# A neighbour sum on one core: the first sort's masks, casts and counts in another order

## The chip, the cores and the metric

The kernel runs on one core of one Trainium2 chip. The metric is the device time of one execution in microseconds (us). The engines are PE (matrix products), DVE (VectorE), ACT (ScalarE), POOL (GpSimd) and SP (here: DMA issue). Each takes its own instructions in order; semaphores join them.

## The reference

```python
def reference(node_features, edge_index_src, edge_index_dst):
    output = np.zeros((4096, 128), dtype=np.float32)
    for i in range(65536):
        output[edge_index_dst[i]] += node_features[edge_index_src[i]]
    return output
```

The edges come in random order. Both index arrays are given as 64-bit integers; the kernel reads them as pairs of 32-bit words.

## The kernel before, in words

The sum is made as dense products. A destination has a block (`dst >> 7`, 32 blocks) and a column in it; a source has a block (`src & 31`, 32 blocks) and a row in it. For a group of four destination blocks and one source block the kernel counts how often each pair (row, destination) occurs: one-hot matrices of 128 x 128 are multiplied on PE (`blocks`, L766), ACT copies the counts to SBUF (`a`), and PE multiplies them with that block of the node features, as a rounded part and a remainder (`product`, L773). Eight groups of 32 source blocks make 32 *slots* of eight source blocks each (loop at L1080). DVE writes the one-hots of the next slot (`onehots`, L757) while PE works on the present one.

So that such blocks can be formed, edges are sorted twice.

*First sort*, by destination block. The 512 edges of each partition are cut into six *lists* (q = 0 to 5) of 22 columns with four lanes each. For a list, DVE writes a one-hot of its blocks (`buckets1`), PE sums its columns (`column_sums1`), DVE scans the sums (`scan`), and PE and ACT count, for each edge, how many edges of its block come before it (`counts` for list 0, `counts_by_two` for the others: a matmul into PSUM, then a ReLU with a bias on ACT, four columns per call of `count`; a seventh call sums the counts to ranks). Then POOL multiplies the one-hot with the edge's word (`spread`, four parts), DVE writes permutation matrices from the ranks (`windows`, four parts), and PE moves the words (`moves`, four parts). The word of an edge is its source block mask (`src_blocks`, `src & 31`) beside a code of source row and destination column (`codes`); ACT casts both into one 32-bit word (`words`, L236), and POOL's `spread` needs the words. The tile that `spread` writes is used by every second list, so list 2 must wait until PE has moved list 0.

*Second sort*, by source block, once per group. Group 0's is done on the way (`keys0`, `payloads0`, `counts0`, `permute0`, `permuted0`), and its result is taken out by ACT as pairs (`pairs0`) and keys (`keys_of_0`) in two parts: the first for slot 0, the second for slots 1 to 3. The other groups' sorts (`pass2`) are hung into the slots by hooks: `at(slot, where, ...)` registers functions and `do(slot, where)` runs them. `PLAN[g]` names eight places for groups 3 to 7: buckets, chunk sums (POOL; with the payloads of the group before), sum before all (a PE matmul into PSUM and a copy on ACT, then POOL masks and folds), repeats, ranks (PE), permutations (DVE), moves (PE), keys (ACT).

Nothing is scheduled by a program: the order of the calls at L436 to L1077, and the hooks, is the order of each engine's queue. Moving a call past calls that use other engines alone changes no queue. DVE's one-hots take their iota out of PSUM (tile `psi`), which is why the iotas are copied there at the start. Dummy matmuls (`keep_busy`) fill some pauses of PE. A PSUM tag with four buffers (`psA`) is shared by counts, ranks, dummy matmuls and blocks.

Of the kernel before, what the change touches and what calls it, by code (L numbers as in the profile page):

```python
# [8 lines left out]
P = 128  # L9
# [19 lines left out]
GROUPS = (4,) * 8  # L29
WARM = 38  # L30
LATE_PAYLOADS = (2, 3, 4, 5, 6)
PLAN = {
# [5 lines left out]
}  # L38
# [48 lines left out]
def _fast(ctx, tc, X, src32, dst32, out, ident, fmax, flag_i, T):  # L87
# [144 lines left out]

    def src_blocks():
        V.tensor_single_scalar(out=sblk_i, in_=s_lo, scalar=31, op=OP.bitwise_and)

# [33 lines left out]
    def oh1q(q):  # L269
        return oh1[q // 2][:, q % 2]  # L270
# [7 lines left out]
    def base_of(j):  # L278

        return j - 1 if j < TURN else TURN + NJ - j  # L280
# [22 lines left out]
    def before_by_two(oh, cum, biases):  # L303

        psc = ps.tile([P, 512], F32, name="psc", tag="psA", bufs=4)
        for i in range(len(biases)):
            at = 2 * i * P
            PE.matmul(out=psc[:, at:at + 2 * P], lhsT=oh[:, 2 * i], rhs=early2[:],  # L308
                      start=True, stop=False)
            PE.matmul(out=psc[:, at + P:at + 2 * P], lhsT=oh[:, 2 * i + 1], rhs=early2[:, :P],  # L310
                      start=False, stop=True)
        for i, bias in enumerate(biases):
            S.activation(out=cum[:, 2 * i:2 * i + 2].rearrange("p j e -> p (j e)"),  # L313
                         in_=psc[:, 2 * i * P:2 * (i + 1) * P], func=RELU, bias=bias)

    def counts_by_two(q):

        cum = sb1.tile([P, NJ, P], BF16, name="cum", tag="oh0" if q == 1 else f"c{q % 2}")
        col = oh1q(q).rearrange("p (j l) b -> p j (l b)", l=4)
        for j0 in range(0, NJ, 4):  # L320
            js = range(j0, min(j0 + 4, NJ))
            before_by_two(col[:, j0:js.stop], cum[:, j0:js.stop],
                          [sums[q][:, base_of(j):base_of(j) + 1] if j else minus[:] for j in js[::2]])
            yield
        psr = ps.tile([P, 512], F32, name="psr", tag="psA", bufs=4)
        for j in range(NJ):
            PE.matmul(out=psr[:, 4 * j:4 * j + 4], lhsT=cum[:, j], rhs=lists[:],
                      start=True, stop=True)
        take_ranks(q, psr)
# [27 lines left out]
    def count(q):  # L357
        next(counting[q], None)

    counting = [counts_by_two(q) if q else counts(q) for q in range(NQ)]  # L360

    def spread(q, w):

        if w == 0:
            v1[q] = sb1.tile([P, NL, NB], F32, name="v1", tag=f"A{q % 2}")
        ts = slice(4 * WIN[w][0], 4 * WIN[w][1])
        G.tensor_tensor(out=v1[q][:, ts], in0=oh1q(q)[:, ts], op=OP.mult,  # L367
                        in1=kab[:, q, ts, None].to_broadcast([P, ts.stop - ts.start, NB]))
# [52 lines left out]
    def finish():  # L421
        for k, res in done:
            rows = sb1.tile([P, 512], F32, name="rows", tag="K0")
            V.transpose(out=rows[:], in_=res[:])
            store_blocks((nc.sync,), rows, k)
        done.clear()

    def leave(k, pso):

        rows = sb1.tile([P, 512], F32, name="rows", tag="K0")  # L430
        V.transpose(out=rows[:], in_=pso[:])
        store_blocks((nc.sync, nc.scalar), rows, k)
# [8 lines left out]
                (3, iota4[:].rearrange("p s k -> p (s k)"))])  # L441
    codes(0, 2)
    scan(0)
    dst_keys(1, 2)
    buckets1(1)
    dst_keys(2, NQ)
    codes(2, NQ)
    src_blocks()
    keys2 = {}
# [42 lines left out]
    def counts0(q):  # L492
        cs = place(q)
        before_by_two(T0["o"][:, cs].rearrange("p c s k -> p c (s k)"),
                      T0["c"][:, cs].rearrange("p c s k -> p c (s k)"),
                      [T0["s"][:, c - 1:c] if c % NH else minus[:]
                       for c in range(cs.start, cs.stop, 2)])

# [37 lines left out]

    def take_pairs(pa, x, s0=0, s1=NB):

        x = x.rearrange("p (a j s u) -> p a j s u", a=2, j=2, u=2)[:, :, :, s0:s1]
        d = pa.rearrange("p (s j a) -> p a j s", j=2, a=2)[:, :, :, s0:s1]  # L540
        S.copy(out=d[:64], in_=x[:64, :, :, :, 0])
        S.copy(out=d[64:], in_=x[64:, ::-1, :, :, 1])

# [16 lines left out]
    def at(slot, where, *fs):  # L560
        hooks.setdefault((slot, where), []).extend(fs)
# [5 lines left out]
    def pass2(g):  # L567
# [149 lines left out]
        if g == 1:  # L717
            at(1, 2, ranks)
            at(1, 3, permutations)
            at(2, 4, lambda: permuted(0), lambda: permuted(1))  # L720
            at(2, 5, quad_keys)
            return buckets, payloads, column_sums, sums_to_each, counts
        if g == 2:
            owed[2] = payloads
            at(2, 0, before_all, masked, folded)
            at(2, 4, repeats, repeats_folded)
            at(5, 0, ranks)
            at(5, 1, permutations)
            at(6, 4, lambda: permuted(0), lambda: permuted(1))
            at(6, 5, quad_keys)  # L730
            return buckets, chunk_sums
# [88 lines left out]

    def pairs0(i):
        if not pairs:
            pairs.append(pairs_tile())
        take_pairs(pairs[0][:], T0["x"][:, :8 * NB], *PARTS0[i])

# [11 lines left out]
    for i, where in ((2, 2), (3, 3)):  # L837
        at(1, where, lambda i=i: x_part(i, 0), lambda i=i: x_part(i, 1))
    count(0)
    count(0)  # L840
    count(0)
    count(0)
    words(0, 1)
    spread(0, 0)
    spread(0, 1)
    spread(0, 2)
    spread(0, 3)
    count(0)
    count(0)
# [4 lines left out]
    spread(1, 1)  # L854
    spread(1, 2)
    spread(1, 3)
    buckets1(2)
    count(1)
    keep_busy(6)
    count(0)  # L860
    column_sums1(2)
# [20 lines left out]
    moves(0, 2)  # L882
    windows(0, 3)
    count(2)
    count(2)
    moves(0, 3)
    moved_blocks(0)
# [10 lines left out]
    count(2)  # L898
    scan(4)
    count(3)  # L900
    count(3)
    moves(1, 1)
    windows(1, 2)
    count(3)
    count(3)
    count(3)
    moves(1, 2)
    windows(1, 3)
# [8 lines left out]
    spread(3, 3)  # L917
    windows(2, 0)
    column_sums1(5)
    moves(2, 0)  # L920
# [24 lines left out]
    spread(4, 3)  # L945
    windows(3, 0)
    scan0(0)
    counts0(0)
    scan0(1)
    counts0(1)  # L950
    moves(3, 0)
    windows(3, 1)
# [4 lines left out]
    count(5)  # L957
    count(5)
    count(5)
    windows(3, 2)  # L960
    count(5)
    moves(3, 2)
    moves(3, 3)
    moved_blocks(3)
    keys0(2)
    sums0(2)
    count(5)
    moved_codes(3)
    spread(5, 0)
    spread(5, 1)  # L970
    spread(5, 2)
    spread(5, 3)
    windows(4, 0)
    moves(4, 0)
    windows(4, 1)
    moves(4, 1)
    count(5)
    scan0(2)
    counts0(2)
    windows(4, 2)  # L980
    windows(4, 3)
    keys0(3)
    moves(4, 2)
    moves(4, 3)
    moved_blocks(4)
    windows(5, 1)
    payloads0(2)
    moved_codes(4)
    windows(5, 0)
    sums0(3)  # L990
    scan0(3)
    counts0(3)
    payloads0(0)
    payloads0(3)
    x_part(0, 0)
    windows(5, 2)
    moves(5, 0)
    moves(5, 1)
    keys0(4)
    moves(5, 2)  # L1000
    payloads0(1)
    windows(5, 3)
    early_ranks()
    payloads0_moved(4)
    sums0(4)
    moves(5, 3)
    moved_blocks(5)
    moved_codes(5)
    earlier0()
    scan0(4)  # L1010
    counts0(4)
    keep_busy(16)
# [5 lines left out]
    permute0(EARLY0[1])  # L1018
    x_part(1, 0)
    counts0(5)  # L1020
    ranks0_apart(place(4))
    permuted0(0, EARLY0)
    ranks0_apart(last0)
    x_part(1, 1)
    payloads0_moved(5)
    permute0(place(4))
    permuted0(1, EARLY0)
    permuted0(0, (place(4),))
    permuted0(1, (place(4),))
    permute0(last0)  # L1030
    permuted0(0, (last0,))
    permuted0(1, (last0,))
    pairs0(0)
    pairs0(1)
    keys_of_0(0)
    second_ranks()
    keep_busy(28)
    buckets_1(0, 12)
    buckets_1(12, NCH)
    keys_of_0(1)  # L1040
    counting_1 = counts_1()
    next(counting_1)
    column_sums_1()
    payloads_1()
    cur, a, pso = first_tiles()
    oh0(0, 4)
    oh0(4, 4)
    sums_1()
    oh0(8, 8)
    oh0(16, 16)  # L1050
    buckets_2()
    chunk_sums_2()
    oh = onehots(1)
    blocks(0, cur, a)
    blocks(1, cur, a)
    next(counting_1, None)
    product(0, 0, a, pso)
# [6 lines left out]
    product(2, 0, a, pso)  # L1064
    product(3, 0, a, pso)
    blocks(4, cur, a)
    blocks(5, cur, a)
    next(counting_1, None)
# [135 lines left out]
```

## Time and profile before

| | |
|---|---|
| median of 3 runs | 258.85 us (258.82 to 258.94) |
| profiled execution | 258.85 us, span of its instructions 257.2 us |
| PE busy | 246.5 us (96%) |
| DVE busy | 227.4 us (88%) |
| ACT busy | 196.1 us (76%) |
| POOL busy | 195.2 us (76%) |
| first sort and group 0's second sort | to about 52 us |
| slots 0 to 31 | about 52 to 252 us |

Busy time is the sum of an engine's instructions; a busy PE may still have matmuls that overlap. Starts in the rows are microseconds from the first instruction of the span. A row of the timeline may merge several instructions of one form ("x9"); then its duration runs from the first one's start to the last one's end.

### The profile page before, as it was taken

The page shows a single profiled execution, that of the slowest core. Times are in us where ns is not written, and L with a number is a line of the kernel's source. Part 1 is how long each engine was busy: PE and PEld are TensorE (multiplying, and loading weights), DVE is VectorE, ACT ScalarE, POOL GpSimd, SP SyncE. Part 2 cuts the span into 40 slices and gives each one's busy share as a digit, 9 for nine tenths or more (in the row PEclk, how much of TensorE's full clock was granted, in tenths as well). Part 3 has the DMA queues.
Part 4 walks back from the last instruction along what each step waited for, and adds up shares of the span by engine and source line. Part 5 has one row for each costly group of instructions (what it writes and reads, how often), then busy time and mean ns, then how long its engine had stood idle before and what let it go on. Part 6 is the DMA issues. An engine that isn't in the chain of part 4 may idle for free.

```text
span 257.2 us, 7399 instructions
## 1 busy us (share of the span) xinstructions
PE 246.5 (96%) x3164; PEld 208.1 (81%) x3164; DVE 227.4 (88%) x165; ACT 196.1 (76%) x426; POOL 195.2 (76%) x211
## 2 busy tenths in 40 slices
PE   7899999899999999989999999999999999999991
PEld 7689999768888888778888878888888788788781
DVE  6987769899999999999999999999999889599701
ACT  6798997778978777767777868697859776888660
POOL 7399999998899999999998999999969930000000
PEclk9999999999999999999999999999999999999997
DMA  5800000000000000220002000100020020002002
GB/s 159 314 21 6 3 4 6 3 0 3 1 3 3 0 3 0 43 41 3 0 8 36 4 1 13 31 3 0 9 36 3 0 43 0 3 1 43 0 1 45
DMA packets 19139, 5.74 MB, mean 22 GB/s; under 512 B 17056, under 2 KB 18592, under 8 KB 19104
## 3 DMA queue, kind: packets, MB, share of 16 engines
q1 hardware_dynamic: 17232, 4.59, 7.5%
q10 hardware_dynamic: 1872, 0.66, 1.1%
q8 instruction: 25, 0.41, 0.7%
q14 instruction: 10, 0.08, 0.1%
HBM read 3.15 MB, written 2.10 MB: 20 GB/s over the span
## 4 chain that ended last, share of the span: by engine, by line
PE 71%; POOL 16%; ACT 7%; DVE 3%; issue 1%; POOLq 0%; DVEq 0%
PE pso L776 36%; PE psa L769 17%; PE psm L393 5%; POOL cum L645 5%; PE ps L676 3%; POOL two L609 3%; POOL v L598 2%; ACT a L771 2%; PE psc L308 2%; PE psw L160 2%; ACT cum L313 2%; POOL cum L652 2%; POOL same L640 1%; POOL cum L654 1%; POOL four L609 1%; PE psc L310 1%
## 5 line engine op out<-in xcount | busy, mean ns | idle before, releaser
L771 ACT CAST a<-psa 128x512 fp32r<-128x512 f32 x256 | 131.8, 606 | 29.7 <-PE psa L769 29.5
L750 DVE TENSOR_TENSOR oh<-psi,keys 128x8192 bf16<-128x8192 uint16 (+3 forms) x43 | 141.4, 3320 | 5.2 <-ACT keys L547 3.6
L776 PE MATMUL pso<-a,xr 128*128 128x512 f32 x512 | 134.0, 404 | 0.0
L776 PEld LDWEIGHTS pso<-a,xr 128*128 128x128 f32 x512 | 91.3, 189 | 16.7 <-ACT a L771 0.2
L769 PEld LDWEIGHTS <-oh 128*128 128x128 bf16 x1024 | 57.7, 98 | 15.1 <-issue 13.5
L769 PE MATMUL psa<-oh 128*128 128x128 bf16 x1024 | 68.7, 220 | 0.4 <-DVE oh L750 0.4
L645 POOL TENSOR_TENSOR cum<-oh,base 128x512 bf16<-128x512 bf16 x36 | 40.6, 1160 | 3.6 <-ACT base L620 3.6
L598 POOL TENSOR_TENSOR v<-oh,sa 128x512 bf16<-128x512 bf16 x42 | 42.6, 1052 | 0.0
L367 POOL TENSOR_TENSOR v<-oh,kab 128x640 f32<-128x640 bf16 (+1 forms) x24 | 32.1, 1374 | 5.3 <-ACT kab L240 4.7
L264 DVE TENSOR_TENSOR p<-psi,rank 128x1520 bf16<-128x1520 uint16 (+3 forms) x24 | 19.3, 841 | 1.7 <-ACT rank L333 1.6
L313 ACT ACTIVATE cum<-psc,sums 128x256 bf16<-128x256 f32 x50 | 20.1, 544 | 0.6 <-PE psc L310 0.6
L609 POOL TENSOR_TENSOR two<-oh 128x512 bf16<-128x512 bf16 x18 | 20.4, 1164 | 0.0
L393 PE MATMUL psm<-v,p 128*128 128x64 bf16 x512 | 17.9, 193 | 0.0
L393 PEld LDWEIGHTS <-p 128*128 128x128 bf16 x512 | 16.5, 98 | 0.2
L308 PE MATMUL psc<-early,oh 128*128 128x256 bf16 x67 | 13.4, 272 | 0.6 <-ACT cum L313 0.6
L264 DVE TENSOR_TENSOR p2a<-psi,rank 128x5760 bf16<-128x5760 uint16 (+2 forms) x7 | 13.0, 1862 | 0.0
L264 DVE TENSOR_TENSOR p2c<-psi,rank 128x5760 bf16<-128x5760 uint16 x4 | 12.6, 3145 | 0.0
L589 DVE TENSOR_TENSOR oh<-psi,sbk 128x3072 bf16<-128x3072 uint16 (+1 forms) x8 | 12.3, 1548 | 0.0
L310 PE MATMUL psc<-early,oh 128*128 128x128 bf16 x67 | 12.2, 218 | 0.0
L652 POOL TENSOR_TENSOR cum<-cum 128x384 int32<-128x384 int32 x12 | 11.9, 1007 | 0.0
L253 POOL TENSOR_TENSOR xr<-xf,xr 128x512 fp32r<-128x512 f32 x8 | 10.0, 1279 | 1.4 <-ACT xr L249 1.4
L609 POOL TENSOR_TENSOR four<-two 128x384 bf16<-128x384 bf16 x12 | 10.7, 917 | 0.0
(122 smaller groups left out, 225.6 us busy)
## 6 DMA issues: line engine op xcount, KB each, us to landing
xf<-in_node_features_dram SPq DMA_DIRECT2D x4, 512.0 KB, 6.2
out_dram<-rows SPq DMA_DIRECT2D x30, 64.0 KB, 1.9
raw<-in_edge_index_src_dram ACTq DMA_DIRECT2D x1, 336.0 KB, 5.5
raw<-in_edge_index_dst_dram SPq DMA_DIRECT2D x1, 336.0 KB, 5.6
raw<-in_edge_index_src_dram ACTq DMA_DIRECT2D x2, 88.0 KB, 2.4
raw<-in_edge_index_dst_dram SPq DMA_DIRECT2D x2, 88.0 KB, 2.6
out_dram<-rows ACTq DMA_DIRECT2D x2, 64.0 KB, 2.4
```

What stands on the lines that cost most here:

```text
L264: V.tensor_tensor(out=dst.rearrange("p i (m k) -> p i m k", k=2), in0=io.rearrange("p i (m k) -> p i m k", k=2), in1=keys2[:, :, None, :]. ...
L308: PE.matmul(out=psc[:, at:at + 2 * P], lhsT=oh[:, 2 * i], rhs=early2[:], start=True, stop=False)
L313: S.activation(out=cum[:, 2 * i:2 * i + 2].rearrange("p j e -> p (j e)"), in_=psc[:, 2 * i * P:2 * (i + 1) * P], func=RELU, bias=bias)
L367: G.tensor_tensor(out=v1[q][:, ts], in0=oh1q(q)[:, ts], op=OP.mult, in1=kab[:, q, ts, None].to_broadcast([P, ts.stop - ts.start, NB]))
L393: PE.matmul(out=psm[q][:, l * 64:(l + 1) * 64], lhsT=p1[:, j, l, :], rhs=v1[q][:, 4 * j + l].bitcast(BF16), start=j == 0 and l == 0, stop= ...
L598: G.tensor_tensor(out=T2["v"][:, c:c + 4], in0=T2["o"][:, c:c + 4], op=OP.mult, in1=sa[:, c:c + 4, None, d0:d0 + 4].to_broadcast([P, 4, NB ...
L609: G.tensor_tensor(out=to[:, js], in0=of[:, js, 0], in1=of[:, js, 1], op=OP.add)
L645: G.tensor_tensor(out=flat("c")[:, c:c + 4], in0=flat("o")[:, c:c + 4], op=OP.mult, in1=T2["b"][:, c // NH, None].to_broadcast([P, 4, P]))
L750: V.tensor_tensor(out=oh[:, i:i + n].rearrange("p n k (m e) -> p n k m e", e=2), op=OP.is_equal, in0=both.to_broadcast(shape), in1=keys2[g ...
L769: PE.matmul(out=psa[:, i * P:(i + 1) * P], lhsT=oh[:, 4 * k + i, 1, :], rhs=oh[:, 4 * k + i, 0, :], start=True, stop=True)
L771: S.copy(out=a[:, k, :], in_=psa[:])
L776: PE.matmul(out=pso[:], lhsT=xr[s // 16][:, s % 16, v, :], rhs=a[:, k, :], start=s == 0 and v == 0, stop=s == NB - 1 and v == 1)
```

## The change

The diff below leaves out the moves of calls that change no engine's queue, and repeats of a pattern. `src_blocks` gets a range of lists and is called for lists 0 and 1 ahead of the first scan. The first `words` call stands ahead of list 0's counts instead of between its fourth and fifth group. Four groups of counts (list 2 and 3, second and last group) use one ReLU per column (`before_by_one`). The first key part of group 0 is made ahead of the second part of the pairs. Several hooks have other places; some of DVE's windows and scans, POOL's payloads of group 0 and the early ranks are swapped with neighbours.

```diff
+SINGLES = ((2, 1), (2, 5), (3, 1), (3, 5))
 PLAN = {
-    3: ((3, 0), (3, 0), (6, 2), (4, 2), (9, 0), (9, 5), (10, 4), (11, 0)),
-    4: ((6, 3), (7, 3), (9, 0), (8, 5), (12, 0), (13, 4), (14, 4), (15, 0)),
-    5: ((11, 0), (11, 2), (13, 3), (13, 5), (16, 3), (17, 1), (18, 1), (18, 4)),
-    6: ((14, 4), (15, 2), (17, 2), (17, 5), (20, 0), (20, 4), (21, 5), (22, 2)),
-    7: ((18, 5), (19, 1), (21, 4), (22, 0), (24, 5), (26, 0), (26, 0), (26, 3)),
+    3: ((3, 0), (4, 0), (6, 2), (4, 2), (9, 0), (9, 5), (10, 4), (11, 0)),
+    4: ((6, 3), (8, 3), (9, 3), (8, 5), (12, 0), (13, 3), (14, 4), (15, 0)),
+    5: ((11, 0), (11, 2), (13, 3), (13, 3), (16, 3), (17, 1), (18, 1), (18, 4)),
+    6: ((14, 4), (16, 0), (17, 2), (17, 5), (20, 0), (20, 4), (22, 1), (22, 4)),
+    7: ((18, 5), (19, 1), (21, 4), (22, 0), (24, 5), (26, 0), (26, 0), (26, 5)),
 }
...
-    def src_blocks():
-        V.tensor_single_scalar(out=sblk_i, in_=s_lo, scalar=31, op=OP.bitwise_and)
+    def src_blocks(a, b):
+        ts = slice(a * NL, b * NL)
+        V.tensor_single_scalar(out=sblk_i[:, ts], in_=s_lo[:, ts], scalar=31, op=OP.bitwise_and)
...
+    def before_by_one(oh, cum, biases):
+
+        psc = ps.tile([P, 512], F32, name="psc", tag="psA", bufs=4)
+        for i, bias in enumerate(biases):
+            PE.matmul(out=psc[:, i * P:(i + 1) * P], lhsT=oh[:, i], rhs=early2[:, :P],
+                      start=True, stop=True)
+        for i, bias in enumerate(biases):
+            S.activation(out=cum[:, i], in_=psc[:, i * P:(i + 1) * P], func=RELU, bias=bias)
...
-            rows = sb1.tile([P, 512], F32, name="rows", tag="K0")
+            rows = sb1.tile([P, 512], F32, name="rows", tag=f"K{k % 2}")
...
     codes(0, 2)
+    src_blocks(0, 2)
+    dst_keys(1, 2)
     scan(0)
-    dst_keys(1, 2)
     buckets1(1)
     dst_keys(2, NQ)
     codes(2, NQ)
-    src_blocks()
+    src_blocks(2, NQ)
...
         if g == 2:
...
-            at(6, 4, lambda: permuted(0), lambda: permuted(1))
-            at(6, 5, quad_keys)
+            at(6, 5, lambda: permuted(0), lambda: permuted(1))
+            at(7, 0, quad_keys)
...
-    count(0)
-    count(0)
-    count(0)
-    count(0)
     words(0, 1)
     spread(0, 0)
...
     spread(0, 3)
+    count(0)
+    count(0)
+    count(0)
+    count(0)
     count(0)
     count(0)
     column_sums1(1)
...
-    scan(4)
...
     windows(2, 0)
+    scan(4)
...
-    payloads0(2)
+    payloads0(1)
...
-    moves(5, 2)
-    payloads0(1)
     early_ranks()
     sums0(4)
+    moves(5, 2)
...
+    payloads0(2)
...
-    pairs0(0)
-    pairs0(1)
+    pairs0(0, (S.copy, None))
+    pairs0(0, (None, S.copy))
     keys_of_0(0)
+    pairs0(1, (S.copy, None))
+    pairs0(1, (None, S.copy))
```

## Rows read from the trace of the kernel before

**Rows 1.** Busy time in three stretches: us, then PE, PEld, DVE, ACT, POOL busy (x), PEclk, DMA share, GB/s

```profile
10.00:20.00 10.00, 8.30 (x203) 7.77 (x201) 9.26 (x13) 8.89 (x26) 9.56 (x8) 1.00 0.32 119
20.00:30.00 10.00, 10.00 (x287) 9.78 (x286) 8.11 (x13) 8.77 (x27) 9.76 (x8) 1.00 0.02 6
130.00:160.00 30.00, 30.00 (x299) 24.70 (x297) 29.39 (x13) 23.62 (x48) 28.72 (x29) 1.00 0.07 13
```

**Rows 2.** Timeline of PE: start, duration, what, [idle before it and what ended that]

```profile
11.33 1.41 PE L353 MATMUL psr<-cum,identb 128*128 128x88 bf16 x32 [1.15 <-ACT cum L348]
12.58 0.40 PE L286 MATMUL pst<-ones,oh 128*128 128x1 bf16 x10
...
18.74 0.27 PE L308 MATMUL psc<-early,oh 128*128 128x256 bf16 x1 [0.56 <-ACT cum L313]
18.85 0.22 PE L310 MATMUL psc<-early,oh 128*128 128x128 bf16 x1
18.90 0.27 PE L308 MATMUL psc<-early,oh 128*128 128x256 bf16 x1
```

**Rows 3.** Timeline of ACT, 6 to 23 us

```profile
6.38 0.22 ACT L205 COPY psi<-iota 128x64 int32<-128x64 int32 x1
7.00 2.42 ACT L348 ACTIVATE cum<-psc,minus 128x512 bf16<-128x512 f32 x4 [0.41 <-PE psc L345]
...
10.06 0.30 ACT L240 ACTIVATE kab<-raw 128x88 bf16<-128x88 uint16 x1 [0.45 <-DVE raw L234]
10.25 1.03 ACT L348 ACTIVATE cum<-psc,minus 128x512 bf16<-128x512 f32 x2
...
13.69 3.39 ACT L313 ACTIVATE cum<-psc,sums 128x256 bf16<-128x256 f32 x9 [0.60 <-PE psc L310]
...
22.85 0.30 ACT L333 CAST rank<-psr 128x176 bf16<-128x176 f32 x1 [0.35 <-PE psr L327]
```

**Rows 4.** Timeline of POOL, start to 32 us

```profile
3.29 0.49 POOL L184 IOTA iota<- 128x128 uint16 x1
...
10.44 10.68 POOL L367 TENSOR_TENSOR v<-oh,kab 128x640 f32<-128x640 bf16 x8 [4.66 <-ACT kab L240]
21.36 10.69 POOL L367 TENSOR_TENSOR v<-oh,kab 128x640 f32<-128x640 bf16 x8 [0.24 <-PE psm L393]
```

**Rows 5.** Timeline of DVE, 3 to 13 us

```profile
3.55 0.34 DVE L221 TENSOR_SCALAR kd<-raw 128x176 uint16<-128x176 uint16 x1 [0.34 <-DMA raw<-in_edge_index_dst_dram]
...
6.48 0.23 DVE L221 TENSOR_SCALAR kd<-raw 128x176 uint16<-128x176 uint16 x1
...
8.36 0.52 DVE L221 TENSOR_SCALAR kd<-raw 128x704 uint16<-128x704 uint16 x1
...
9.60 0.43 DVE L234 TENSOR_SCALAR raw<-raw 128x528 uint16<-128x528 uint16 x1
...
10.06 3.13 DVE L264 TENSOR_TENSOR oh<-psi,kd 128x2816 bf16<-128x2816 uint16 x2
```

**Rows 6.** Timelines of ACT and DVE at the start of the slots

```profile
49.88 0.23 ACT L542 CAST pairs<-ps 64x32 bf16<-64x32 f32 x1
...
50.91 0.71 ACT L547 CAST keys<-pairs 128x128 uint16<-128x128 uint8 x2
...
49.05 1.81 DVE L589 TENSOR_TENSOR oh<-psi,sbk 128x1536 bf16<-128x1536 uint16 x2
51.24 1.29 DVE L750 TENSOR_TENSOR oh<-psi,keys 128x1024 bf16<-128x1024 uint16 x2 [0.38 <-ACT keys L547]
```

**Rows 7.** Timelines of PE, POOL and DVE in slots 9 and 12

```profile
110.64 0.49 PE L618 MATMUL psb<-four,before 128*128 128x256 bf16 x3 [0.95 <-POOL four L609]
...
129.30 0.35 PE L662 MATMUL psr<-cum,identb 128*128 128x96 bf16 x4
...
127.04 1.67 POOL L654 TENSOR_TENSOR cum<-cum 128x384 int32<-128x384 int32 x2
...
105.05 4.38 DVE L750 TENSOR_TENSOR oh<-psi,keys 128x8192 bf16<-128x8192 uint16 x1
```

More of the change, by code (lines that the diff above doesn't have):

```diff
@@ L305, in before_by_two @@
         psc = ps.tile([P, 512], F32, name="psc", tag="psA", bufs=4)
+        biases = biases[::2]
         for i in range(len(biases)):
@@ L321, in counts_by_two @@
             js = range(j0, min(j0 + 4, NJ))
-            before_by_two(col[:, j0:js.stop], cum[:, j0:js.stop],
-                          [sums[q][:, base_of(j):base_of(j) + 1] if j else minus[:] for j in js[::2]])
+            (before_by_one if (q, j0 // 4) in SINGLES else before_by_two)(
+                col[:, j0:js.stop], cum[:, j0:js.stop],
+                [sums[q][:, base_of(j):base_of(j) + 1] if j else minus[:] for j in js])
             yield
@@ L360, in _fast, with spread @@
     counting = [counts_by_two(q) if q else counts(q) for q in range(NQ)]
-    def spread(q, w):
+    def spread(q, w, engine=G):
         if w == 0:
@@ L366, in spread @@
         ts = slice(4 * WIN[w][0], 4 * WIN[w][1])
-        G.tensor_tensor(out=v1[q][:, ts], in0=oh1q(q)[:, ts], op=OP.mult,
+        engine.tensor_tensor(out=v1[q][:, ts], in0=oh1q(q)[:, ts], op=OP.mult,
                         in1=kab[:, q, ts, None].to_broadcast([P, ts.stop - ts.start, NB]))
@@ L428, in leave @@
     def leave(k, pso):
-        rows = sb1.tile([P, 512], F32, name="rows", tag="K0")
+        rows = sb1.tile([P, 512], F32, name="rows", tag=f"K{k % 2}")
         V.transpose(out=rows[:], in_=pso[:])
@@ L496, in counts0 @@
                       [T0["s"][:, c - 1:c] if c % NH else minus[:]
-                       for c in range(cs.start, cs.stop, 2)])
+                       for c in range(cs.start, cs.stop)])
     def ranks0(cs, psr, halves=1):
@@ L535, in permuted0, with take_pairs @@
             T0["x0"] = True
-    def take_pairs(pa, x, s0=0, s1=NB):
+    def take_pairs(pa, x, s0=0, s1=NB, halves=(S.copy, S.copy)):
         x = x.rearrange("p (a j s u) -> p a j s u", a=2, j=2, u=2)[:, :, :, s0:s1]
         d = pa.rearrange("p (s j a) -> p a j s", j=2, a=2)[:, :, :, s0:s1]
-        S.copy(out=d[:64], in_=x[:64, :, :, :, 0])
-        S.copy(out=d[64:], in_=x[64:, ::-1, :, :, 1])
+        if halves[0]:
+            halves[0](out=d[:64], in_=x[:64, :, :, :, 0])
+        if halves[1]:
+            halves[1](out=d[64:], in_=x[64:, ::-1, :, :, 1])
     def put_keys(k, pa, s0=0, s1=NB):
@@ L718, in pass2 @@
             at(1, 2, ranks)
-            at(1, 3, permutations)
-            at(2, 4, lambda: permuted(0), lambda: permuted(1))
+            at(1, 2, permutations)
+            at(2, 3, lambda: permuted(0), lambda: permuted(1))
             at(2, 5, quad_keys)
@@ L819, in _fast, with pairs0 @@
     PARTS0 = ((0, NB // 4), (NB // 4, NB))
-    def pairs0(i):
+    def pairs0(i, halves=(S.copy, S.copy)):
         if not pairs:
             pairs.append(pairs_tile())
-        take_pairs(pairs[0][:], T0["x"][:, :8 * NB], *PARTS0[i])
+        take_pairs(pairs[0][:], T0["x"][:, :8 * NB], *PARTS0[i], halves)
     def keys_of_0(i):
@@ L855, in _fast @@
     spread(1, 2)
+    keep_busy(6)
     spread(1, 3)
+    count(1)
+    count(0)
     buckets1(2)
-    count(1)
-    keep_busy(6)
-    count(0)
     column_sums1(2)
@@ L882, in _fast @@
     moves(0, 2)
-    windows(0, 3)
     count(2)
     count(2)
+    windows(0, 3)
     moves(0, 3)
@@ L902, in _fast @@
     moves(1, 1)
-    windows(1, 2)
     count(3)
@@ L906, in _fast @@
     count(3)
+    windows(1, 2)
     moves(1, 2)
@@ L945, in _fast @@
     spread(4, 3)
-    windows(3, 0)
     scan0(0)
@@ L950, in _fast @@
     counts0(1)
+    windows(3, 0)
     moves(3, 0)
@@ L958, in _fast @@
     count(5)
+    windows(3, 2)
     count(5)
-    windows(3, 2)
     count(5)
@@ L964, in _fast @@
     moved_blocks(3)
+    moved_codes(3)
     keys0(2)
@@ L967, in _fast @@
     count(5)
-    moved_codes(3)
     spread(5, 0)
@@ L971, in _fast @@
     spread(5, 2)
-    spread(5, 3)
     windows(4, 0)
     moves(4, 0)
+    spread(5, 3)
     windows(4, 1)
@@ L979, in _fast @@
     counts0(2)
+    windows(4, 3)
     windows(4, 2)
-    windows(4, 3)
+    moves(4, 2)
     keys0(3)
-    moves(4, 2)
     moves(4, 3)
+    windows(5, 0)
+    payloads0(1)
     moved_blocks(4)
     windows(5, 1)
-    payloads0(2)
-    moved_codes(4)
-    windows(5, 0)
     sums0(3)
@@ L993, in _fast @@
     payloads0(0)
+    moved_codes(4)
     payloads0(3)
@@ L999, in _fast @@
     keys0(4)
+    early_ranks()
+    sums0(4)
     moves(5, 2)
-    payloads0(1)
     windows(5, 3)
-    early_ranks()
     payloads0_moved(4)
-    sums0(4)
     moves(5, 3)
     moved_blocks(5)
-    moved_codes(5)
+    payloads0(2)
     earlier0()
     scan0(4)
+    moved_codes(5)
     counts0(4)
@@ L1019, in _fast @@
     x_part(1, 0)
+    ranks0_apart(place(4))
     counts0(5)
-    ranks0_apart(place(4))
     permuted0(0, EARLY0)
     ranks0_apart(last0)
-    x_part(1, 1)
     payloads0_moved(5)
     permute0(place(4))
+    x_part(1, 1)
     permuted0(1, EARLY0)
+    permute0(last0)
     permuted0(0, (place(4),))
     permuted0(1, (place(4),))
-    permute0(last0)
     permuted0(0, (last0,))
     permuted0(1, (last0,))
-    pairs0(0)
-    pairs0(1)
+    pairs0(0, (S.copy, None))
+    cur, a, pso = first_tiles()
+    pairs0(0, (None, S.copy))
     keys_of_0(0)
-    second_ranks()
+    pairs0(1, (S.copy, None))
+    pairs0(1, (None, S.copy))
     keep_busy(28)
@@ L1039, in _fast @@
     buckets_1(12, NCH)
+    payloads_1()
     keys_of_0(1)
-    counting_1 = counts_1()
-    next(counting_1)
     column_sums_1()
-    payloads_1()
-    cur, a, pso = first_tiles()
     oh0(0, 4)
@@ L1048, in _fast @@
     sums_1()
+    counting_1 = counts_1()
+    next(counting_1)
     oh0(8, 8)
     oh0(16, 16)
+    second_ranks()
     buckets_2()
     chunk_sums_2()
-    oh = onehots(1)
     blocks(0, cur, a)
     blocks(1, cur, a)
+    oh = onehots(1)
     next(counting_1, None)
@@ L1065, in _fast @@
     product(3, 0, a, pso)
+    blocks(5, cur, a)
     blocks(4, cur, a)
-    blocks(5, cur, a)
     next(counting_1, None)
```

## The prediction

> **What bounds the kernel now.** I read the busy time by stretches first. In the stretch of the first sort from 10 to 30 us PE is busy nearly throughout, ACT and POOL almost as much, DVE a little less [rows 1]: no engine has a large reserve, and a wait that PE loses there comes off the time. In the steady slots (130 to 160 us) PE is busy all 30 us while the others are not [rows 1]. So from about 60 us on the time is PE's work, and a change can gain only by letting PE start the slots earlier or by removing a wait of PE inside them. The chain of waits says the same by its last part (alternating one-hot blocks and products of PE to the end).
>
> Then I looked for PE's own idle time. The reader should see three places. PE waits 1.15 us for the last ReLU of list 0's counts and starts their sum at 11.33 [rows 2]. At 18.74 it waits 0.56 us for a PSUM buffer that ACT still reads [rows 2]. In slot 9, at 110.64, it waits 0.95 us for POOL's chunk sums [rows 7]. The rest of its idle time lies in the hand-over from the sort to the slots before slot 1, where PE, ACT and DVE answer each other.
>
> Why was ACT late at 11.33? It began list 0's counts at 7.00, then stood before the second word cast until 10.06, waiting 0.45 us for the source blocks that DVE masked for all six lists at 9.60; only then came the last two ReLUs, which end at 10.25 + 1.03 = 11.28 [rows 3, 5]. POOL could not begin its first spread before that cast either and stood 4.66 us, until 10.44 [rows 4].
>
> **The change, part by part.**
>
> A, *masking apart and words first*. The mask for lists 0 and 1 is one DVE instruction of 176 columns; the nearest row of that width took 0.23 us [rows 5]. It and the moved key shift fall into the time in which DVE waits for PE's column sums anyway; before, the key shift stood behind the scan of those, at 6.48 [rows 5]. So the one-hot of list 1 follows the scan at once and starts about 0.3 us earlier than before. The two casts on ACT follow the last copy (6.38 + 0.22), near 6.6 and 6.8, and the first count ReLU still starts at 7.00, because PE's first sum is not ready before [rows 3]. After that six ReLUs follow at the pitch of that row, (2.42 - 0.69)/3 = 0.57: the last starts at 9.87 and, half as wide, takes 1.03 - 0.57 = 0.46, so it ends at 10.33 instead of 11.28: 0.95 us less for PE, which then starts at 10.38. Is PE stopped by what comes next? Its 32 matmuls take 12.58 - 11.33 = 1.25 us, to 11.63, then it wants the one-hot of list 2. Before, that ended near 10.06 + 1.6 = 11.66; 0.3 us earlier by the above and 0.1 by the shorter mask (352 columns of the 528 that took 0.43) makes 11.25, 0.4 us of cover.
>
> That cover has a price to meet. POOL's first spread now starts near 7.2, 3.3 us earlier, beside DVE's four index instructions (8.36 to 10.03 before, 8.05 to 9.6 now), where POOL was idle before [rows 4, 5]. What this does to DVE the trace does not show for these sizes. Lower bound: nothing. Nearest row: the same key shift took 0.34 us at 3.55 beside a POOL iota and 0.23 alone, 0.11 more [rows 4, 5]. Upper bound: each of the four waits for a whole spread, 10.68/8 = 1.33 us [rows 4]. I take the first instruction waiting for the spread in flight (7.2 + 1.33 - 8.05, about 0.45, which the iota row's 0.11 times four also gives): 0.05 more than the cover. A is worth 0.90 us.
>
> The Trainium skill (SBUF — State Buffer, Who interferes with whom) says that VectorE and GpSimd share a port pair held for a whole instruction, taken by VectorE's copies and tensor-scalar operations in their two-port modes and by operations with two SBUF inputs, the later one blocking fully. All four index instructions have only SBUF operands, so by that rule the sum loses up to what the rival below prices; the iota row agrees with a block in kind, with 0.11 us, not with its full length.
>
> POOL's own 3.3 us are not gained: its third list reuses the tile of list 0 and starts when PE has read that out (21.36, released by PE's moves [rows 4]). So POOL stands still for some 2 us instead and stays as much earlier as PE does.
>
> B, *one column per ReLU in four groups*. On PE a pair of columns costs 0.11 + 0.05 = 0.16 us (18.74, 18.85, 18.90), two single ones 0.05 each, so 0.055 less per pair [rows 2]. Six pairs are replaced. The two in (2,1) lie ahead of the wait at 18.74 and only lengthen it; four pairs count: 0.22 us. On ACT twelve ReLUs of 128 columns replace six of 256. None of that width with such a bias is shown. Ends: half of the 256-column pitch, (3.39 - 0.50)/8 = 0.36 [rows 3], that is 0.18 and no extra cost, up to the same 0.36 and 2.2 us more. On the line through 0.36 (256) and 0.57 (512 columns) 128 comes to 0.25, 12 x 0.25 - 6 x 0.36 = 0.84 us more; I take that. ACT's idle time hides it: 10 - 8.77 = 1.23 us in 20 to 30 us, of which 0.35 is the wait at 22.85 [rows 1, 3].
>
> C, *keys of the first slot before the second part of the pairs*. At 49.88 ACT ends the first part, then makes the larger second part, and the keys follow at 50.91 [rows 6]. Now the first keys follow at once, near 50.13, and are there at 50.45. DVE waited 0.38 us for them at 51.24 [rows 6]; it is free at 49.05 + 1.81 = 50.86. Slot 0's one-hots use these keys alone. DVE and with it the first blocks come 0.35 us earlier.
>
> D, *PSUM sum of group 4 at (9,3) instead of (9,0)*. The 0.95 us wait in slot 9 goes, since the sum is issued behind most of that slot's work. What is late next? The one-hots of slot 9 end at 105.05 + 4.38 = 109.43, before PE would want them at 109.69. The ranks of group 4 in slot 12 start at 129.30, and POOL's fold, which they need, ends at 127.04 + 1.67 = 128.71 [rows 7]. POOL's order is unchanged and it has no pause, so PE can gain only 129.30 - 128.71 - 0.05 (the hand-over seen at 110.64) = 0.54 us.
>
> The remaining moves cost nothing in my sum: windows, scans and payloads swapped within DVE's and POOL's queues have the same instructions and their releasers are earlier still; the early ranks ahead of moves (5,2) shift PE work inside a stretch that DVE ends; the payload that is now last on POOL is done before DVE's second permutation that PE awaits anyway. If that cover failed, one such swap would cost a window or payload, about 1 us. The two row tiles have no wait to remove. DMAs keep their number and queues.
>
> Sum: 0.90 + 0.22 + 0.35 + 0.54 = 2.01 us less. The profiled execution took 258.85 us, span 257.2 and 1.6 around it, and is itself the median of the three runs. Predicted: 256.8 us.
>
> **The rivals.** *DVE and POOL exclude each other (slower).* From 8.05 on each index instruction waits for a spread and the next spread slips in between: 0.45 + 3 x 1.33 = 4.4 us. The train ends at 14.0, the one-hot of list 2 at 15.7, and PE's column sums start there instead of at 12.58: 3.2 us late where I have 0.90 early. Time: 258.85 + 3.2 - 0.22 - 0.35 - 0.54 = 260.9. It turns slower once those column sums start after 13.7, that is from about two such waits on. For it: the one-hots that DVE runs beside POOL take their iota from PSUM, and these four, with SBUF operands alone, ran while POOL was idle. Against it: the iota row shows 0.11. That is the case by the skill's rule above.
>
> *ACT is the bound of lists 2 and 3.* The 0.84 us of B come on the path and its 0.22 do not: 256.8 + 1.06 = 257.9. For: ACT's row from 13.69 runs without a pause. Against: it waited for PE at 22.85. The Trainium skill (ScalarE: Activation LUTs, What ACT_TABLE_LOAD costs) gives an activation with a pointer bias a larger fixed part; an estimate by it is 0.29 us per 128 columns but 0.40 per 256, where the row shows 0.36, so I stay with the row.
>
> *Slot 9's gain is handed back* to DVE, whose one-hots have only 0.26 us to spare there: 257.4.
>
> *The early words push the counts back*: if the mask is late, ACT stands with all counts behind the cast and A is nothing: 257.7.
>
> *Nothing arrives*: DVE's contiguous tail before the slots swallows A and B, and C and D are met by another wait: 258.8.
>
> **How the numbers follow.** Forecast 0.53, ACT 0.10, slot 9 handed back 0.08, words late 0.06, nothing 0.06, exclusion 0.17. Below 0.2% (0.5 us) a measurement of this kernel can't tell a change from none. So faster 0.77, same 0.06, slower 0.17. The likeliest case's own range is 256.0 to 257.5; the range that leaves out most of the exclusion case and little else is 255.8 to 259.4.
>
> **What would show it.** The sum of list 0's counts on PE starts at 10.4; the first spread near 7.2; the third list's first spread about 1 us earlier than 21.36, with a pause of POOL before it. DVE's index instructions after 8 us tell A: durations up to 0.5 us over those of before fit the forecast, more than 1 us on each is the exclusion case. The one-column ReLUs' pitch is 0.25. Slot 0's first one-hot comes 1.5 us earlier, PE has no wait in slot 9 and a short one or none in slot 12. I am wrong if PE's column sums of list 2 start after 12.6, or if the slots' end is not as much earlier as the first one-hot plus half a microsecond.

## The result: 1.3% slower, and the profile after

The changed kernel took 261.87 us (median of 6 runs, 261.85 to 262.87) against 258.89 for the kernel before on the same chip: a ratio of 1.0126, 95% interval 1.011 to 1.0142. I had predicted 256.8 us with a range to 259.4. The profiled execution shown here took 262.55 us. In it the first counts began 0.3 us later than in most runs (7.31 instead of 7.00), so positions after 7 us are read as differences between rows, not as absolute gains.

The first sign that I had named is DVE's four index instructions behind 8 us (the key shift L222, the code masks L229 and L231, the source block mask L236; timeline of DVE of the changed kernel: start, duration, what, idle before). The last row belongs to part C.

```profile
8.17 0.55 DVE L222 TENSOR_SCALAR kd<-raw 128x704 uint16<-128x704 uint16 x1
8.64 1.40 DVE L229 TENSOR_SCALAR raw<-raw 128x352 uint16<-128x352 uint16 x1
10.07 1.47 DVE L231 SCALAR_TENSOR_TENSOR raw<-raw 128x352 uint16<-128x352 uint16 x1
11.47 1.83 DVE L236 TENSOR_SCALAR raw<-raw 128x352 uint16<-128x352 uint16 x1
13.22 0.19 DVE L302 TENSOR_TENSOR_SCAN sums<-carry,pst 128x23 f32<-128x23 bf16 x1
13.33 3.12 DVE L266 TENSOR_TENSOR oh<-psi,kd 128x2816 bf16<-128x2816 uint16 x2
...
54.66 1.27 DVE L766 TENSOR_TENSOR oh<-psi,keys 128x1024 bf16<-128x1024 uint16 x2
```

POOL's spreads stand beside them (timeline of POOL, same kernel):

```profile
7.07 1.27 POOL L380 TENSOR_TENSOR v<-oh,kab 128x640 f32<-128x640 bf16 x1 [1.26 <-ACT kab L242]
8.30 1.55 POOL L380 TENSOR_TENSOR v<-oh,kab 128x640 f32<-128x640 bf16 x1
9.80 1.36 POOL L380 TENSOR_TENSOR v<-oh,kab 128x640 f32<-128x640 bf16 x1
11.12 1.97 POOL L380 TENSOR_TENSOR v<-oh,kab 128x896 f32<-128x896 bf16 x1
13.06 1.36 POOL L380 TENSOR_TENSOR v<-oh,kab 128x640 f32<-128x640 bf16 x1
...
24.94 2.49 POOL L380 TENSOR_TENSOR v<-oh,kab 128x640 f32<-128x640 bf16 x2 [6.42 <-ACT cum L316]
```

Read the ends of the rows together. Spreads end at 8.34, 9.85, 11.16 and 13.09; the index instructions end at 10.04, 11.54 and 13.30, 0.19, 0.38 and 0.21 us after a spread's end and not before. The key shift ahead of them (L222) came while the first spread was nearly over and lost only 0.03 us. Each index instruction gets one turn between two spreads. The one-hot of list 2, which began at 10.06 [rows 5], begins at 13.33. POOL, 3.4 us early, does not keep that: it stands still for 6.42 us before list 2, whose first spread begins at 24.94 where it was 21.36 [rows 4].

On PE (timeline, same kernel) the sum of list 0's counts is early as forecast (10.73 for 11.33 before), and then the wait that I had put at nothing is 2.83 us; before, that row (12.58) had no wait [rows 2]:

```profile
10.73 1.41 PE L366 MATMUL psr<-cum,identb 128*128 128x88 bf16 x32 [0.24 <-ACT cum L361]
...
14.98 0.42 PE L288 MATMUL pst<-ones,oh 128*128 128x1 bf16 x10 [2.83 <-DVE oh L266]
...
16.21 0.42 PE L311 MATMUL psc<-early,oh 128*128 128x256 bf16 x1
16.42 0.31 PE L313 MATMUL psc<-early,oh 128*128 128x128 bf16 x1
16.53 0.42 PE L311 MATMUL psc<-early,oh 128*128 128x256 bf16 x1
...
117.01 0.49 PE L634 MATMUL psb<-four,before 128*128 128x256 bf16 x3
...
132.24 0.33 PE L678 MATMUL psr<-cum,identb 128*128 128x96 bf16 x4 [0.17 <-POOL cum L670]
```

After that wait the pairs of count matmuls follow each other at 0.32 us (16.21, 16.53) where [rows 2] has 0.16 (18.74, 18.90). The busy times by stretch say why (columns as in [rows 1]): the granted clock, 1.00 in these stretches before, is 0.50 from 15 to 20 us, the lower of its two levels.

```profile
10.00:15.00 5.00, 1.93 (x40) 1.65 (x38) 4.97 (x6) 2.04 (x7) 5.00 (x4) 0.88 0.61 227
15.00:20.00 5.00, 5.00 (x82) 4.44 (x83) 3.64 (x6) 3.55 (x10) 3.52 (x3) 0.50 0.02 3
20.00:30.00 10.00, 10.00 (x279) 9.74 (x277) 9.69 (x12) 9.30 (x30) 5.06 (x4) 0.97 0.02 4
```

The row at 117.01 is the PSUM sum of group 4, now without a wait; at 132.24 PE waits 0.17 us for POOL's fold: part D did what it should. One more row differs that I had given no price (DMA issues at the end: queue, count, size, median us from issue to landing), of the kernel before,

```profile
out_dram<-rows SPq DMA_DIRECT2D x2, 64.0 KB, 2.2
out_dram<-rows ACTq DMA_DIRECT2D x2, 64.0 KB, 2.4
```

and of the changed kernel:

```profile
out_dram<-rows SPq DMA_DIRECT2D x2, 64.0 KB, 2.7
out_dram<-rows ACTq DMA_DIRECT2D x2, 64.0 KB, 2.9
```

### The profile page after: what moved, and what is told of

Its sections match the earlier page's. It is cut to its first block, busy times and chain, and to the rows that moved or that the text cites. A ratio compares the mean times of both kernels' runs of the same rounds, so it can differ in the third digit from the quotient of the medians.

```text
span 260.9 us, 7405 instructions
## 1 busy us (share of the span) xinstructions
PE 248.8 (95%) x3163; PEld 209.8 (80%) x3164; DVE 230.7 (88%) x166; ACT 197.3 (76%) x432; POOL 196.2 (75%) x211
## 4 chain that ended last, share of the span: by engine, by line
PE 60%; POOL 23%; DVE 6%; ACT 6%; issue 2%; DMA 1%; SPq 0%; POOLq 0%; DVEq 0%; ACTq 0%
PE pso L792 31%; PE psa L785 14%; POOL cum L661 8%; PE psm L406 5%; POOL v L614 4%; PE psc L311 3%; POOL two L625 3%; ACT a L787 2%; PE ps L692 2%; POOL cum L668 2%; POOL same L656 2%; POOL cum L670 2%; PE psc L313 1%; DVE oh L266 1%; ACT cum L316 1%
## 5 line engine op out<-in xcount | busy, mean ns | idle before, releaser
L380 POOL TENSOR_TENSOR v<-oh,kab 128x640 f32<-128x640 bf16 (+1 forms) x24 | 32.9, 1405 | 8.4 <-ACT cum L316 6.4
L316 ACT ACTIVATE cum<-psc,sums 128x256 bf16<-128x256 f32 x44 | 17.9, 534 | 4.4 <-PE psc L313 2.3
L668 POOL TENSOR_TENSOR cum<-cum 128x384 int32<-128x384 int32 x12 | 11.9, 1015 | 0.0
L556 ACT CAST pairs<-ps 64x128 bf16<-64x128 f32 (+2 forms) x9 | 3.7, 411 | 9.6 <-PE ps L692 8.0
```

Of the source, the lines that this page charges most:

```text
L380: engine.tensor_tensor(out=v1[q][:, ts], in0=oh1q(q)[:, ts], op=OP.mult, in1=kab[:, q, ts, None].to_broadcast([P, ts.stop - ts.start, NB]))
```

## The experiments

Twelve kernels ran, each beside the kernel before (258.89 to 258.91). A is the split mask with early words, B the one-column ReLUs, C the moved keys, D the new order of the sort's hooks; E is a part that I had passed over, the output rows' buffer.

| run | what it is | us | ratio to before, 95% |
|---|---|---|---|
| words_behind | after, words behind all counts | 258.10 | 0.9961 (0.9947 to 0.9976) |
| words_first_alone | before + A | 262.21 | 1.011 (1.0073 to 1.0147) |
| probe | before + 8 DVE instructions | 264.73 (one run) | |
| after_busy | after + dummy matmuls in the hole | 261.35 | 1.0087 (1.0061 to 1.0112) |
| words_between | after, words at the old place | 258.34 | 0.9979 (0.997 to 0.9989) |
| words_between_pairs | the same, without B | 258.14 | 0.997 (0.996 to 0.9981) |
| hooks_alone | before + D | 258.42 | 0.9982 (0.9972 to 0.9992) |
| keys_alone | before + C | 258.49 | 0.9985 (0.9975 to 0.9995) |
| rows_alone | before + E | 259.63 | 1.0026 (1.0017 to 1.0036) |
| singles_alone | before + B | 259.23 | 1.0008 (0.9999 to 1.0018) |
| best_k0 | words_between_pairs without E | 257.48 | 0.9944 (0.9927 to 0.9961) |
| best_padded | words_between_pairs, K1 moved by 64 bytes | 257.47 | 0.994 (0.9924 to 0.9957) |

**Do the early spreads cause it?** Theory 1: an index instruction and a spread exclude each other, and POOL's early start makes them meet. Theory 2: casting the words ahead of the counts is late by itself, wherever POOL stands.

```diff
-    words(0, 1)
-    spread(0, 0)
...
     count(0)
...
     count(0)
+    words(0, 1)
+    spread(0, 0)
...
     column_sums1(1)
```

All six count groups now stand ahead of the words (the cut is marked by dots: four spreads move along).

> The changed kernel with one thing put elsewhere: list 0's words are cast behind all six groups of list 0's counts instead of ahead of them, so POOL's first spread starts near 10.6 us, after DVE's index instructions, as it did before the change. Theory 1 (DVE's instructions on SBUF operands alone and POOL's spreads take turns): L229, L231 and L236 take 0.3 to 0.5 us again instead of 1.40, 1.47 and 1.83, PE's column sums of list 2 start near 11.7, and as the other parts gain 0.3 (keys), 0.5 (slots 9 to 12) and 0.9 (head), the time is 256.6 to 257.3. Theory 2 (the loss lies in the one-column ReLUs, the swaps or the hooks): the time stays within 0.5 us of the changed kernel's 261.9.

With the spreads at 11.13 the three instructions took again what they took before (timelines of DVE and POOL of words_behind):

```profile
8.60 0.34 DVE L229 TENSOR_SCALAR raw<-raw 128x352 uint16<-128x352 uint16 x1
8.97 0.52 DVE L231 SCALAR_TENSOR_TENSOR raw<-raw 128x352 uint16<-128x352 uint16 x1
9.41 0.34 DVE L236 TENSOR_SCALAR raw<-raw 128x352 uint16<-128x352 uint16 x1
```

```profile
11.13 19.67 POOL L380 TENSOR_TENSOR v<-oh,kab 128x640 f32<-128x640 bf16 x15 [5.35 <-ACT kab L242]
```

3.77 us less than the changed kernel: theory 2's 261.9 is out. But 258.10 is 0.8 above theory 1's upper end. Part of that is visible: POOL now runs without a pause. B and E, which theory 1 had left out, are measured alone below; their 0.34 and 0.74 us are enough for the rest.

Part A on the kernel before, alone:

> The kernel before with part A alone: the mask for lists 0 and 1 apart, the key shift ahead of the scan, the words of list 0 cast ahead of its counts. Theory 1 (turns of DVE and POOL): all of the loss and none of the gains of the other parts, 262.3 to 263.2, with the three index instructions at 1.4 us or more. Theory 2 (the loss lies in other parts): A alone is not slower, 257.9 to 258.9.

262.21, 0.09 below its range: A by itself costs 3.3 us, and the three index instructions take 1.40, 1.47 and 1.83 us again. Its four runs lie between 261.79 and 263.01, which takes in the changed kernel's 261.87: A alone is enough for the whole loss.

**What kind of exclusion is it?** Eight extra DVE instructions were put behind list 3's one-hot, in the middle of POOL's spreads, two of each kind: a mask with 256 columns from and to SBUF, a mask with 128 columns out of PSUM, a comparison of two SBUF operands with 256 columns, and a comparison of a PSUM and an SBUF operand with 128.

```diff
     buckets1(3)
+    probe()
     count(1)
```

> The kernel before with eight extra DVE instructions behind the one-hot of list 3, about 13 to 16 us, while POOL spreads lists 0 and 1 without a pause; their results are used by nothing. Two each of: a mask of 256 columns from SBUF to SBUF; a mask of 128 columns from PSUM to SBUF; a comparison of 256 columns with both inputs in SBUF; a comparison of 128 columns with one input in PSUM and one in SBUF. Theory 1 (turns): the first and third kind take 0.3 us and up to a spread's 1.3 us more, the second and fourth stay near 0.2 to 0.3 us. Rival (any DVE work on SBUF is slowed beside POOL, in proportion): all four are longer by a like factor. The time of the whole is not the question; some 2 to 6 us longer.

Timeline of DVE, then of POOL, of that kernel:

```profile
13.10 1.13 DVE L241 TENSOR_SCALAR scr<-raw 128x256 uint16<-128x256 uint16 x1
14.26 1.62 DVE L241 TENSOR_SCALAR scr<-raw 128x256 uint16<-128x256 uint16 x1
15.80 0.47 DVE L243 TENSOR_SCALAR scr<-psi 128x128 uint16<-128x128 uint16 x2
16.19 0.98 DVE L245 TENSOR_TENSOR scr<-raw,scr 128x256 uint16<-128x256 uint16 x1
17.20 1.23 DVE L245 TENSOR_TENSOR scr<-raw,scr 128x256 uint16<-128x256 uint16 x1
18.36 0.47 DVE L247 TENSOR_TENSOR scr<-psi,raw 128x128 uint16<-128x128 uint16 x2
```

```profile
12.88 1.26 POOL L380 TENSOR_TENSOR v<-oh,kab 128x640 f32<-128x640 bf16 x1
14.10 1.69 POOL L380 TENSOR_TENSOR v<-oh,kab 128x896 f32<-128x896 bf16 x1
15.76 1.26 POOL L380 TENSOR_TENSOR v<-oh,kab 128x640 f32<-128x640 bf16 x1
16.98 1.31 POOL L380 TENSOR_TENSOR v<-oh,kab 128x640 f32<-128x640 bf16 x1
```

The two masks end at 14.23 and 15.88, the spreads at 14.14 and 15.79: 0.09 us later both times. The longer spread (1.69) makes the longer mask (1.62), so it is a wait for the spread in flight and no slowing by a factor. The comparisons of two SBUF operands end 0.15 and 0.14 us behind a spread. With one operand in PSUM two instructions take 0.47 us together and wait for nothing. The Trainium skill (SBUF — State Buffer, Who interferes with whom) states both, the port pair held for a whole instruction and the exemption of operations with at most one SBUF input outside the two-port modes; these rows agree. They add that the two engines alternate: the next spread, though issued back to back, lets the waiting DVE instruction through first.

**Does the lower clock matter?** Fifty dummy matmuls fill PE's hole in the changed kernel.

> The changed kernel with 50 more dummy matmuls on PE between the sum of list 0's counts and the column sums of list 2, where PE waits 2.8 us for DVE. Rival theory (PE's fall to the lower granted clock between 12 and 20 us costs a part of the loss by itself): matmul pairs from 15.6 us run at 0.16 instead of 0.32 us, the first one-hot of the slots comes 1 to 1.5 us earlier and the time is 260.4 to 261.0. Theory 1 in its pure form (DVE's delay passes on whole, the clock costs nothing): 261.6 to 262.0, since DVE or ACT are the bound there anyway.

Busy times by stretch of that kernel, 15 to 20 us:

```profile
15.00:20.00 5.00, 4.99 (x134) 4.81 (x135) 5.00 (x8) 3.87 (x11) 3.55 (x3) 1.00 0.02 3
```

The clock stays at 1.00 and PE does 134 matmuls there instead of 82, but the time falls by only 0.52 us, between the two expectations. PE then waits 0.7 us for a PSUM buffer that ACT's ReLUs still read, a wait that the changed kernel does not have. So about 0.5 us of the loss is the clock; what is left of A's 3.3 goes with the late one-hot of list 2.

**Where should the words stand, and what are B, C and D worth?**

```diff
+    count(0)
+    count(0)
+    count(0)
+    count(0)
     words(0, 1)
...
-    count(0)
-    count(0)
-    count(0)
-    count(0)
     count(0)
     count(0)
```

> The changed kernel with list 0's words and their two spreads issued between the fourth and the fifth count group, where the kernel before had them; the mask split, the one-column ReLUs, the moved keys and the new plan stay. By the theory of turns (an index instruction with both operands in SBUF and a POOL spread wait for each other's end) POOL starts near 9.8, when the four index instructions are done, so they take 0.34, 0.52 and 0.34 us again and the one-hot of list 2 ends near 10.9; POOL is 1.3 us ahead of the kernel with the words behind all counts, whose wait at 18.16 (0.82) goes. Time 257.2 to 257.9. By the rival (casting the words ahead of any later count group is what costs, whatever DVE does) it stays above 259.

> The kernel words_between with no one-column ReLUs (every count group by two columns per ReLU, as before). If PE's waits for the counts of list 3 (0.18 and 0.23 us in the kernel with the words behind the counts) come from ScalarE at 0.25 us per 128 columns, they go and the time is 0.2 to 0.5 us below words_between. If the one-column ReLUs gain the 0.22 us on PE that was forecast, it is 0.2 us above words_between.

> The kernel before with only the new plan and the moved hooks of the first sort. If the gain of slot 9 is its own, the wait of 0.95 us in slot 9 goes, slots 8 and 12 give 0.4 us back, and the time is 258.3 to 258.5. If it was there only because the changed kernel came to the sort in another state, the time stays at 258.9.

> The kernel before with only the first list's keys moved ahead of the second pairs part. If the keys' wait (0.38 us) stood on the path that sets the end, the time is 258.5 to 258.6. If what comes after waits for POOL or ScalarE anyway, it stays at 258.9.

With the words at their old place DVE's index instructions end at 9.75, POOL's first spread begins at 9.87 and nothing meets. D alone gave 0.47 us, as expected, and C alone 0.40, 0.01 more than its range. But words_between at 258.34 missed its range by 0.4, and words_between_pairs came to 258.14 although its slots stand 1.50 us earlier than before, up to the last. The first block matmuls of slot 31 (timeline of PE), before and in words_between_pairs:

```profile
244.45 1.07 PE L769 MATMUL psa<-oh 128*128 128x128 bf16 x16
```

```profile
242.95 1.07 PE L785 MATMUL psa<-oh 128*128 128x128 bf16 x16
```

Half of that was lost behind the last slot, in the last store.

**The last store.** In the changed kernel the output rows alternate between the buffers K0 and K1. The trace's packet records of the eight output stores (2048 packets of 128 bytes each; mean ns a packet, in order):

| kernel | 1 | 2 | 3 | 4 | 5 | 6 | 7 | 8 |
|---|---|---|---|---|---|---|---|---|
| before | 11.7 | 11.7 | 11.7 | 11.8 | 11.6 | 11.9 | 11.9 | 12.2 |
| after | 11.7 | 13.1 | 11.7 | 13.3 | 11.7 | 13.4 | 12.0 | 13.5 |
| best_padded | 11.7 | 11.6 | 11.7 | 11.9 | 11.7 | 11.9 | 12.0 | 12.2 |

In the compiled programs K0 begins at 91776 bytes of each partition and K1 at 93888, 64 bytes off a multiple of 128.

```diff
-    kd = sb1.tile([P, NQ, NL, 2], U16, name="kd", tag="K0")
+    kd = sb1.tile([P, NQ * NL * 2 + 32], U16, name="kd", tag="K0")
+    kd = kd[:, :NQ * NL * 2].rearrange("p (q t w) -> p q t w", q=NQ, w=2)
```

> The kernel before with only the tile of the output rows alternating between the buffers K0 and K1, as in the changed kernel. In the profiles of the changed kernel the packets of every second output store (those from K1) took 13.1 to 13.5 ns and those from K0 11.7, and the last store landed 2.7 and 2.9 us after its issues instead of 2.2 and 2.4. If the buffer is the cause, this kernel's last store takes 2.7 and 2.9 and the time is 259.3 to 259.6. If the longer store comes from the other edits of the change (another place in time, other transfers beside it), it takes 2.2 and 2.4 and the time is 258.9.

> The kernel words_between_pairs with the output rows in K0 throughout, as in the kernel before: the mask split with the words after the fourth count group, the moved keys and the new plan, no one-column ReLUs. If the buffer of the rows is what kept words_between_pairs (slots 1.5 us earlier) at only 0.75 us below before, the time is 257.4 to 257.7; if not, it stays at 258.1.

> The kernel words_between_pairs with the rows alternating between K0 and K1 as in the changed kernel, but with K0 64 bytes longer, so that K1 begins at 93952 instead of 93888 bytes of each partition, a multiple of 128 as K0's 91776. If the 128-byte packets are slow because they begin 64 bytes off such a multiple, all stores take 11.7 ns a packet, the last store 2.2 and 2.4 us, and the time is that of best_k0. If the alternation itself, or a second buffer, is the cause, the packets from K1 stay at 13 ns and the time at 258.1.

The last DMA issues of rows_alone, then of best_padded:

```profile
out_dram<-rows SPq DMA_DIRECT2D x2, 64.0 KB, 2.7
out_dram<-rows ACTq DMA_DIRECT2D x2, 64.0 KB, 2.9
```

```profile
out_dram<-rows SPq DMA_DIRECT2D x2, 64.0 KB, 2.2
out_dram<-rows ACTq DMA_DIRECT2D x2, 64.0 KB, 2.4
```

Two came out as expected, rows_alone 0.03 us above its range. The buffer alone costs 0.74 us: 0.5 in the landing, under 0.1 in the slots, 0.2 after the last packet that the trace doesn't explain. Still alternating, but with K1 (and every tile behind it) moved by 64 bytes, nothing is lost: it is the address. Of the 2048 packets of a store from K1 539 to 739 took 14 ns or more in the changed kernel, of a store from K0 at most 30.

The Trainium skill (DMA: Bandwidth & Descriptors, How a descriptor splits into AXI transactions) says that a transaction must start at a multiple of 256 bytes, and that a descriptor which does not starts its first one at the multiple below. An estimate by it, if each packet is one descriptor: every second packet from K1 crosses such a multiple and needs two transactions, none from K0 or the moved K1 does. The traces agree on which buffer is slow; the slow packets are fewer than half, so that this is how the time is lost is not shown.

**B alone.**

> The kernel before with only the four count groups by one column per ReLU. If the price on ScalarE (0.25 us per 128 columns instead of 0.36 per 256) comes through to PE as words_between against words_between_pairs showed (0.30 us at slot 0), the time is 259.0 to 259.2. If the 0.22 us on PE that the prediction counted is gained, it is 258.6 to 258.7.

259.23, 0.03 above its range: a price of 0.34 us by the medians, at the edge of what the interval can tell. Where it arises the profile shows. PE's sum of list 3 (timeline of PE), in the kernel before and then in singles_alone:

```profile
27.63 0.69 PE L327 MATMUL psr<-lists,cum 128*128 128x4 bf16 x22
```

```profile
27.56 1.12 PE L339 MATMUL psr<-lists,cum 128*128 128x4 bf16 x22
```

The one-column ReLUs that it waits for (timeline of ACT of singles_alone) end at 28.45:

```profile
27.41 0.36 ACT L413 ACTIVATE sbk<-psm 128x128 bf16<-128x128 f32 x1
27.56 0.36 ACT L416 CAST sa<-psm 128x128 bf16<-128x128 f32 x1
27.71 0.74 ACT L325 ACTIVATE cum<-psc,sums 128x128 bf16<-128x128 f32 x2
```

PE arrives 0.07 us earlier and leaves 0.36 us later (its next count matmul starts at 28.54 instead of 28.18), and slot 0's first one-hot is as much later, 51.60 instead of 51.24.

## Why the prediction was wrong, step by step

**A, the failed step.** It is the sentence "I take the first instruction waiting for the spread in flight (7.2 + 1.33 - 8.05, about 0.45, which the iota row's 0.11 times four also gives): 0.05 more than the cover." The first instruction lost 0.03 us, the three after it 1.06, 0.95 and 1.49 (words_behind against after): 3.5 us. The mechanism stood in the text as the rival on exclusion, at 0.17, with 260.9 us; three whole waits came as it said. It had PE's column sums 3.2 us late where they are 2.40 (14.98 for 12.58); the lower clock (0.5) and E (0.74), which it did not count, and B (0.34 of loss for 0.22 of gain) bring its 260.9 to the 261.9 measured.

The row that I held against the rival was misread. I took its 0.11 us for the price of two engines beside each other. But the iota ends at 3.29 + 0.49 = 3.78 [rows 4], 0.23 us after the key shift's start at 3.55 [rows 5], which is just what the shift takes alone [rows 5]: a whole wait could not show as more, and the shift ends 0.11 us behind the iota as the probe's masks end 0.09 us behind a spread. In the 14 kernels of this case the shift starts between 3.27 and 3.56 and ends at 3.87 to 3.90 every time, behind the iota's end at 3.78 or 3.79. The longest (timeline of DVE of words_between_pairs):

```profile
3.27 0.62 DVE L222 TENSOR_SCALAR kd<-raw 128x176 uint16<-128x176 uint16 x1
```

So the row was a case of the rival, with little left to wait for. Another that spoke for it was in the same text, that DVE's one-hots beside POOL take their iota from PSUM; the probe shows that one operand there is enough not to wait. The PE half of A was right: the sum of list 0 starts at 10.73 with counts 0.31 late, 10.42 without that (10.43 in words_first_alone), for a forecast of 10.38.

**B.** The pitch of 0.25 was right; "ACT's idle time hides it" was not. I set 0.84 us against the idle time of the whole stretch, but the last one-column group of list 3 stands directly ahead of PE's sum. B is 0.34 us of loss by the medians, not 0.22 of gain: the rival *ACT is the bound* was right in kind, but less than half of its 0.84 us came on the path.

**C and D** were right: 0.40 for 0.35, 0.47 for 0.54. With D alone slot 9's first block matmul comes 1.08 us earlier than before (109.89 for 110.97). By slot 12 0.50 is left (129.15 for 129.65), since the sum itself now stands in slot 9 and POOL's fold is awaited. Within this gain slot 8 comes 0.37 us later (103.91 for 103.54), behind ACT's pairs and keys of a moved permutation (from 98.10 instead of 96.19), which I had not counted. DVE takes nothing of it back, so *slot 9's gain handed back* is out.

**E** I had put at nothing: "The two row tiles have no wait to remove. DMAs keep their number and queues." Both are true; what changed was their source address, 0.74 us.

The parts alone come to 3.30 + 0.34 + 0.74 - 0.40 - 0.47 = 3.51 us, the change to 2.98. A's four runs differ among themselves by 1.2 us, so whether the parts overlap can't be told. A's split mask with the words at their old place, C, D and the remaining swaps (best_k0) give 258.89 - 257.48 = 1.41 us of the 2.01 predicted. Slot 0's first one-hot starts there at 50.26, with C alone at 50.77: about 0.5 us is left for the split mask and the swaps together, which no run separates.

## What to carry to other kernels

Before starting a POOL stream earlier, list what DVE does in the time it moves into: the masks and two-input operations with SBUF operands alone waited here for the POOL instruction in flight, each time, and behind a full queue that is nearly a whole one. Judge a row of two engines side by side by where the instructions end, not by how much longer one took. Idle time of a helper engine hides a cost only where it lies ahead of the wait in question, not in the stretch's sum. When a DMA reads a tile in 128-byte packets, compare addresses: here a start at a multiple of 128 bytes made the last store 0.5 us shorter.

## What the runs showed of the hardware that I had not expected

- In the first sort DVE and POOL took turns, one instruction each, although POOL's spreads are issued without a gap: a mask of 0.34 us became 1.83, while eight spreads together took 11.45 us instead of 10.68.
- 64 bytes of a buffer's address made packets of 128 bytes 13.1 to 13.5 ns long in the mean instead of 11.6 to 12.2, and the last store 0.5 us longer.
- A DVE key shift that takes 0.23 us alone ended 0.1 us behind POOL's iota in all 14 kernels, wherever it began, and took up to 0.62.
- After a hole of 2.83 us on PE the granted clock from 15 to 20 us was 0.50 instead of 1.00; filling it with useless matmuls brought back 0.5 us.
